# A two-layer MLP by Strassen-Winograd: one SBUF layout for both layers, twelve early quads, sums kept in DRAM

## Chip, core and metric

One core of one Trainium2 chip. The metric is the device time of one execution in microseconds (us); before: a median of 2001.36 over three runs (1999.55 to 2003.11).

## What is computed

One conformer convolution module and one squared-ReLU MLP, both with a residual, on 2048 tokens of width 1024 in fp32:

```python
def reference(x, ...):                     # x: (1, 2048, 1024)
    h = rms_norm(x, mix_norm[0])
    x = x + conformer_conv(h, ...)         # ends in ... @ w_out + b_out
    x = x + squared_relu_mlp(rms_norm(x, mlp_norm[0]), mlp_w1[0], mlp_w2[0])
    return x

def squared_relu_mlp(x, w1, w2):           # w1: 1024 x 4096, w2: 4096 x 1024
    return jnp.square(jax.nn.relu(x @ w1)) @ w2
```

## The kernel before

Everything is held transposed: features on the 128 partitions, 512 tokens a tile. The 2048 tokens are four blocks of 512. Every fp32 operand of a product is split into a high half (ACT casts it) and a low half (a subtraction on DVE or POOL), and a product takes three matmuls for each 128 of its depth: high by high, high by low, low by high. A tile of both halves is `act` (activations) or `wq` (weights, L559 to L563, from a raw tile `rawq`, 128 x 1024, 512 KB).

Blocks 0 and 1 are done first, with plain matmuls (the front, up to L531, 1188 us of the span); the conv outputs of blocks 2 and 3 are left in DRAM. The rest works on blocks 2 and 3 together, in phases, each with an SBUF pool of its own that takes the place of the one before (`reopened`):

- **Projection** (`project_spilled`): 16 loads of the conv outputs (`s`), each split; then for each block and each of eight row tiles a load of `w_out`, 24 matmuls into a `px` bank, and x + conv result goes to DRAM (`x2d`).
- **Norms**: `norm_first` and `norm_second` are generators. `poll()` in the matmul loop steps them, so that their instructions come between products; a number that they yield is how many of these turns they pause. They reload `x2d`, scale it and make seven forms (B11, B21, B22, T1 to T4) for Strassen-Winograd's products over the two blocks and the two halves of the width.
- **First layer**: 16 `Quad`s. Each takes a 2 x 2 block of `w1` tiles and makes seven products P1 to P7, 12 matmuls each, in PSUM banks `px` (3), `py` (2), `pz` (2); sums of products pass through squared ReLU and go to DRAM as forms of the hidden layer (`hB`, `hT`). The first `EARLY` quads do P1 and P2, which need only B11 and B21, while `norm_second` runs; P1's result goes to DRAM (`leave`) and comes back (`resume`) with P2's.
- **Second layer**: for g in 0..7 and o in 0, 1 (16 steps): `hidden(g)` loads and splits 14 tiles, `blocks(g, o)` loads four tiles of `w2` and forms seven weights, then 14 products of 6 matmuls. The results are added to sixteen accumulators `acc` in SBUF, by POOL (six adds a step, L850) and DVE (two, L864). After g = 7 they are stored to `outT`.

The order of instructions on an engine is set by a scheduler when the program is built, from the order of the code, priorities, and when buffers come free; every engine, and the DMA queue of SP, then runs its list in order. So a load that stands behind a store waits for what the store waits for.

Of the kernel before, what the change touches and what calls it, by code (L numbers as in the profile page):

```python
# [31 lines left out]
P = 128  # L32
# [6 lines left out]
T = 512  # L39
# [9 lines left out]
EARLY = 5  # L49
# [10 lines left out]
def conformer_mlp(ctx: ExitStack, tc, xT, w_in, w_out, w1, w2, vecs, conv_w, outT):  # L60
# [127 lines left out]

    class Stats:
# [9 lines left out]
        def buf(self, name, dtype=F32):  # L199
            tag, bufs = ("lstat", 3) if self.ln else ("stat", 4)  # L200
            return sb.tile([P, T], dtype, name=name, tag=tag, bufs=bufs)
# [394 lines left out]
    x2d = [[dram.tile([P, T], F32, name=f"x2_{b}_{m}") for m in range(KD)] for b in range(2)]  # L596
# [6 lines left out]
    def project_spilled(b, ss, norm):  # L603
        st = Stats(False)
        for m in range(KD):
            w = load_plain(w_out[m])
# [5 lines left out]
            nc.sync.dma_start(x2d[b][m], o)  # L612
            st.add_square(m, o)
        return spawn(norm(st))

    def x_normed(b, m, rs, xn):
        x = loaded(x2d[b][m], "x2")
# [8 lines left out]
    def norm_first(st):  # L626
        rs = yield from st.rstd_later(WAIT, GAP)
        for k in range(HK):
            n0[k] = acts.tile([P, 2, T], F32, name="n0", tag="act", bufs=n_act)
# [43 lines left out]
    class Quad:  # L673
# [12 lines left out]
        def sums(self):  # L686
            a2 = raw_wq(w1[2 * self.q + 1])
            a11, a12, a21, self.a22 = self.a1[:, :T], self.a1[:, T:], a2[:, :T], a2[:, T:]
            self.s1, self.s2 = small(sb, "s1", 1), small(sb, "s2", 1)
# [5 lines left out]
        def p1(self):  # L695
            product(self.x, w_split(self.a1[:, :T], nc.vector), form["B11"])
            self.c1 = small(wts, "p1", 2)
# [13 lines left out]
        def resume(self):  # L711
            self.high()
            self.c1 = small(wts, "p1", 2)
# [4 lines left out]
        def copied(self, ps, name):  # L718
            t = small(sb, name, 2)
# [24 lines left out]
        def p4(self):  # L744
# [7 lines left out]
            t1, t2, t4 = [small(sb, n, 1) for n in ("h1", "h2", "h4")]  # L752
# [14 lines left out]
    phase.close()  # L767
    sb, n_raw = reopened("first", phase), 4
# [24 lines left out]
    phase.close()  # L793
    sb = reopened("second", phase)
    ORDER = (("A11", "B11"), ("A12", "B21"), ("S2", "T2"), ("S1", "T1"), ("S3", "T3"), ("S4", "B22"), ("A22", "T4"))
    acc = [[None] * KD for _ in range(2)]

    def copied(ps, name, pool_=None):
        t = small(pool_ or sb, name, 2)
        nc.scalar.copy(t, ps)  # L800
        return t
# [29 lines left out]
    for g in range(NG):  # L831
        for o in range(2):
            if g == 0:
                for b in range(2):
                    for m in range(4 * o, 4 * o + 4, 2):
                        t = acts.tile([P, 2, T], F32, name="acc", tag="act", bufs=n_act)
                        for i in range(2):
                            acc[b][m + i] = t[:, i, :]
                            nc.sync.dma_start(acc[b][m + i], x2d[b][m + i])
# [3 lines left out]
            p1 = [copied(t, "p1", wts) for t in px]  # L843
            both(py, "P2", h["B21"], ws["A12"])
            c = [added(t, p) for t, p in zip(py, p1)]

            def add(x, n, ts):
                for i, t in enumerate(ts):
                    a = acc[n][4 * o + 2 * i + x]
                    nc.gpsimd.tensor_add(a, a, t)  # L850

            add(0, 0, c)
            both(px, "P6", h["T2"], ws["S2"], first=False)
            u2 = [copied(t, "u2") for t in px]
            both(pz, "P5", h["T1"], ws["S1"])
            p5 = [copied(t, "p5") for t in pz]
            both(px, "P7", h["T3"], ws["S3"], first=False)
            add(1, 1, [added(t, p) for t, p in zip(px, p5)])
            both(pz, "P3", h["B22"], ws["S4"], first=False)
            add(0, 1, [added(t, p) for t, p in zip(pz, u2)])  # L860
            both(px, "P4", h["T4"], ws["A22"], first=False)
            for i, t in enumerate(px):
                a = acc[0][4 * o + 2 * i + 1]
                nc.vector.tensor_add(a, a, t)  # L864
            if g == NG - 1:
                for m in range(4 * o, 4 * o + 4):
                    for b in range(2):
                        nc.sync.dma_start(outT[m * P : (m + 1) * P, (b + 2) * T : (b + 3) * T], acc[b][m])
# [51 lines left out]
```

## Time and profile before

| | |
|---|---|
| median of 3 runs | 2001.36 us |
| profiled execution | 2001.76 us, span 1999.6 us |
| busy: TensorE, DVE, ACT, POOL | 94%, 82%, 41%, 38% |
| mean granted TensorE clock | 0.978 of full speed |
| DMA | 264.60 MB, 132 GB/s over the span |

TensorE is the engine with most work. A row of the timeline gives the start, the time, the engine, the line, what is written and read, and in brackets how long the engine was idle before and what released it.

### The profile page before, as it was taken

Reading aid. Unit: us, or ns where it says so; the run is one execution under the profiler, and the core shown is the slowest. Engines: PE = TensorE matmul, PEld = TensorE weight load, DVE = VectorE, ACT = ScalarE, POOL = GpSimd, SP = SyncE. Lnnn points to the kernel's source line nnn. Section 1 sums busy time; section 2 is a strip of 40 time slices with the busy share of each in tenths; the row PEclk is TensorE's granted clock in tenths of the full one; section 3 lists DMA queues with packets and bytes.
Section 4 is the critical chain, followed back from the end, with each engine's and each line's share of the span. In section 5 each row is a group of like instructions: output and inputs, shape, how many; then the busy total and the mean of one; then the engine's idle time right before and its main releaser. Section 6 shows DMA issues by size and latency. Waiting matters only on the chain.

```text
span 1999.6 us, 23532 instructions
## 1 busy us (share of the span) xinstructions
PE 1883.3 (94%) x8192; PEld 1538.8 (77%) x8192; DVE 1640.7 (82%) x2315; ACT 820.4 (41%) x1322; POOL 751.3 (38%) x471
## 2 busy tenths in 40 slices
PE   8999999999899999999999977968999986999998
PEld 6888888888678778788888766856788875777777
DVE  7999999999999999799999733585656556899994
ACT  5323125243353333433231523443455554555552
POOL 2356322644445520000000003434444544676765
PEclk9999999999999999999999998988999998999999
DMA  5123222422224333643121456635545456444342
GB/s 198 64 88 116 89 76 75 143 96 96 89 89 138 106 111 111 219 143 99 62 70 64 155 188 224 225 129 189 191 142 169 157 193 205 156 143 143 122 136 84
DMA packets 135286, 264.60 MB, mean 132 GB/s; under 512 B 12928, under 2 KB 39680, under 8 KB 135168
## 3 DMA queue, kind: packets, MB, share of 16 engines
q1 hardware_dynamic: 135168, 263.11, 40.1%
q8 instruction: 64, 1.05, 0.2%
q14 instruction: 54, 0.44, 0.1%
HBM read 202.78 MB, written 60.28 MB: 132 GB/s over the span
## 4 chain that ended last, share of the span: by engine, by line
PE 40%; DVE 8%; issue 5%; DMA 4%; POOL 2%; ACT 1%; SPq 0%; POOLq 0%; DVEq 0%; ACTq 0%
PE ps L163 16%; PE px L586 11%; PE pz L586 5%; PE px L163 5%; PE py L586 3%; DVE act L93 2%; DVE wq L562 2%; DVE cc L665 1%; DMA rawq<-in_w 1%; DMA w2r<-in_w 1%; POOL s L814 1%; DVE acc L864 1%; ACT act L92 0%; POOL wq L562 0%; DMA s<-conv 0%
## 5 line engine op out<-in xcount | busy, mean ns | idle before, releaser
L163 PE MATMUL ps<-act,w 128*128 128x512 f32 x2880 | 666.2, 391 | 10.3 <-ACT w L92 7.9
L163 PEld LDWEIGHTS ps<-act,w 128*128 128x128 f32 x2880 | 541.4, 188 | 126.8 <-ACT w L92 7.9
L163 PE MATMUL ps<-hid,w 128*128 128x512 f32 x1920 | 445.6, 392 | 4.8 <-DVE hid L93 4.4
L163 PEld LDWEIGHTS ps<-hid,w 128*128 128x128 f32 x1920 | 360.0, 188 | 85.3 <-DVE hid L93 7.2
L586 PE MATMUL px<-act,wq 128*128 128x512 f32 x1536 | 375.5, 397 | 48.0 <-ACT wq L561 24.9
L586 PEld LDWEIGHTS px<-act,wq 128*128 128x128 f32 x1536 | 291.8, 191 | 116.8 <-ACT wq L561 25.8
L93 POOL TENSOR_TENSOR w<-raw,w 128x1024 fp32r<-128x1024 f32 x90 | 217.8, 2420 | 289.4 <-ACT w L92 282.7
L349 DVE SCALAR_TENSOR_TENSOR cacc<-hc,cw,cacc 128x512 f32<-128x512 f32 x464 | 324.7, 749 | 1.4
L349 DVE SCALAR_TENSOR_TENSOR cacc<-h,cw,cacc 128x512 f32<-128x512 f32 x464 | 316.8, 747 | 0.0
L92 ACT CAST w<-raw 128x1024 fp32r<-128x1024 f32 (+1 forms) x150 | 155.1, 1035 | 288.9 <-PE ps L163 284.3
L586 PE MATMUL pz<-act,wq 128*128 128x512 f32 x768 | 186.3, 392 | 2.1 <-ACT p L722 2.1
L850 POOL TENSOR_TENSOR acc<-acc,cc 128x512 f32<-128x512 f32 x96 | 149.5, 1575 | 89.1 <-DVE cc L665 77.2
L586 PEld LDWEIGHTS pz<-act,wq 128*128 128x128 f32 x768 | 145.4, 189 | 33.0 <-ACT p L722 2.5
L562 POOL TENSOR_TENSOR wq<-rawq,wq 128x512 fp32r<-128x512 f32 x48 | 72.8, 1517 | 148.7 <-ACT wq L561 144.8
L93 DVE TENSOR_TENSOR act<-ld,act 128x512 fp32r<-128x512 f32 x112 | 106.2, 971 | 15.8 <-ACT act L92 15.3
L562 DVE TENSOR_TENSOR wq<-rawq,wq 128x512 fp32r<-128x512 f32 x64 | 58.6, 917 | 70.0 <-ACT wq L561 70.0
L437 DVE TENSOR_TENSOR h<-h,ps 128x512 f32<-128x512 f32 x128 | 87.0, 684 | 31.1 <-PE ps L163 29.4
L163 PE MATMUL px<-act,wq 128*128 128x512 f32 x384 | 90.5, 398 | 22.8 <-ACT wq L561 22.8
L212 POOL TENSOR_TENSOR acc<-acc,hc 128x512 f32<-128x512 f32 x12 | 14.0, 1165 | 251.7 <-DVE hc L349 201.5
L586 PE MATMUL py<-act,wq 128*128 128x512 f32 x384 | 95.3, 398 | 13.7 <-DVE cc L665 13.7
L424 ACT ACTIVATE relu<-ps 128x512 f32<-128x512 f32 x64 | 38.2, 597 | 162.8 <-PE ps L163 159.1
L163 PEld LDWEIGHTS px<-act,wq 128*128 128x128 f32 x384 | 73.8, 193 | 39.0 <-ACT wq L561 23.3
(128 smaller groups left out, 2012.7 us busy)
## 6 DMA issues: line engine op xcount, KB each, us to landing
raw<-in_w SPq DMA_DIRECT2D x104, 512.0 KB, 3.6
rawq<-in_w SPq DMA_DIRECT2D x37, 512.0 KB, 4.2
xt<-in_xT SPq DMA_DIRECT2D x64, 256.0 KB, 3.6
ld<-hT SPq DMA_DIRECT2D x64, 256.0 KB, 3.0
w2r<-in_w SPq DMA_DIRECT2D x64, 256.0 KB, 3.8
raw<-in_w_in SPq DMA_DIRECT2D x30, 512.0 KB, 3.2
hB<-cc SPq DMA_DIRECT2D x48, 256.0 KB, 3.6
ld<-hB SPq DMA_DIRECT2D x48, 256.0 KB, 3.8
```

What stands on the lines that cost most here:

```text
L92: nc.scalar.copy(hl[:, 0, :], src)
L93: eng.tensor_sub(hl[:, 1, :], src, hl[:, 0, :].bitcast(F32))
L163: nc.tensor.matmul(ps, lhsT=w(k, a), rhs=x[:, b, :], start=k == 0 and i == 0, stop=k == len(xs) - 1 and i == 2,)
L349: nc.vector.scalar_tensor_tensor(out, h[:, k : k + T], cw[:, j, k : k + 1], acc, ALU.mult, ALU.add)
L424: nc.scalar.activation(r, ps, AF.Relu)
L437: nc.vector.tensor_add(x2[i][m], x2[i][m], ps)
L562: eng.tensor_sub(hl[:, 1, :], src, hl[:, 0, :].bitcast(F32))
L586: nc.tensor.matmul(ps, lhsT=hl[:, a, off + k * P : off + (k + 1) * P], rhs=x[:, b, :], start=first and k == 0 and i == 0, stop=k == n - 1 ...
L665: nc.vector.tensor_add(out, ps, t)
L814: nc.gpsimd.tensor_add(s1, a21, a22)
L850: nc.gpsimd.tensor_add(a, a, t)
L864: nc.vector.tensor_add(a, a, t)
```

## The change

Five things change, all behind the front:

- `EARLY` goes from 5 to 12. `norm_second` pauses four turns instead of one, writes B22 over B11, and makes all low halves on DVE (before, T1 and B22 on POOL).
- The pools of the three phases become one set (`low`, `wts`, `high`, `mid`, `top`, `sb2`) that is open throughout. Small tiles share a tag of six buffers, `rawq` has four, and results that wait for a later product share four buffers of 128 x 2 x 512 (`pair`).
- The first weights of the projection and the first eight `s` tiles are loaded with priority; the other eight come after the first block's projection in the code.
- The second layer loads `w2` as two tiles of 512 KB instead of four of 256 KB; its first step forms its weight sums on DVE.
- The sums stay in DRAM (`x2_pairs`): for g < 7 GpSimd issues DMAs that add a pair tile to them (`accum_op`), four a step, and no accumulator is in SBUF; P4 is copied out of PSUM by ACT. For g = 7 the sum so far is loaded (`base`), DVE and POOL add the last results, and it is stored. The descriptor scratch space of DMAs is halved (8192).

```diff
-EARLY = 5
+EARLY = 12
...
-    wts = reopened("wts", ctx)
-    forms = ctx.enter_context(ExitStack())
-    acts = reopened("acts", forms)
-    n_act, n_raw, n_tmp = 29, 2, 2
-    phase = ctx.enter_context(ExitStack())
-    sb = reopened("projection", phase)
+    low, wts, high, mid, top, sb = [reopened(n, ctx) for n in ("low", "wts", "high", "mid", "top", "sb2")]
...
+    def mid_tile(name):
+        return mid.tile([P, T], F32, name=name, tag="m", bufs=6)
...
+    def pair(name):
+        return sb.tile([P, 2, T], F32, name=name, tag="pair", bufs=4)
...
     def raw_wq(src):
-        t = sb.tile([P, 2 * T], F32, name="rawq", tag="rawq", bufs=n_raw)
-        nc.sync.dma_start(t, src)
+        t = top.tile([P, 2 * T], F32, name="rawq", tag="rawq", bufs=4)
+        nc.sync.dma_start(t if src.shape == t.shape else t.rearrange("p (s q c) -> p s q c", s=2, q=2), src)
         return t
...
     def norm_second(st):
         rs = yield from st.rstd_later(WAIT, GAP)
         for k in range(HK):
-            b12 = x_normed(1, k, rs, small(sb, "n1", 3))
-            b22 = x_normed(1, HK + k, rs, small(sb, "n1", 3))
             b11, b21 = n0[k][:, 0, :], n0[k][:, 1, :]
-            t1 = small(sb, "t1", 1)
+            b12 = x_normed(1, k, rs, mid_tile("n1"))
+            t1, t2 = mid_tile("t1"), mid_tile("t2")
             nc.vector.tensor_sub(t1, b12, b11)
-            t2 = small(sb, "t2", 1)
+            b22 = x_normed(1, HK + k, rs, b11)
             nc.vector.tensor_sub(t2, b22, t1)
             form["T2"][k] = act_split(t2)
-            form["T1"][k] = act_split(t1, nc.gpsimd)
-            yield 1
+            form["T1"][k] = act_split(t1)
+            yield 4
             nc.vector.tensor_sub(b12, b22, b12)
             form["T3"][k] = act_split(b12)
-            form["B22"][k] = act_split(b22, nc.gpsimd)
             nc.vector.tensor_sub(b21, b21, t2)
-            form["T4"][k] = act_split(b21)
-            yield 1
-
-    ss = [[act_split(loaded(conv_out[j][i], "s")) for j in range(KD)] for i in range(2)]
-    ta = project_spilled(0, ss[0], norm_first)
-    tb = project_spilled(1, ss[1], norm_second)
+            yield 4
+        for k in range(HK):
+            form["B22"][k] = act_split(n0[k][:, 0, :])
+            form["T4"][k] = act_split(n0[k][:, 1, :])
+            yield 4
+
+    with tc.high_priority():
+        w0 = load_plain(w_out[0])
+        ss = [act_split(loaded(conv_out[j][0], "s")) for j in range(KD)]
+    ta = project_spilled(0, ss, norm_first, w0)
+    ss = [act_split(loaded(conv_out[j][1], "s")) for j in range(KD)]
+    tb = project_spilled(1, ss, norm_second)
     finish(ta)
...
-        a11, a12, a21, a22 = [small(sb, "w2r", 8) for _ in range(4)]
-        for i, t in enumerate((a11, a12, a21, a22)):
-            nc.sync.dma_start(t.rearrange("p (q c) -> p q c", q=2), w2[g, o][:, i])
-        s1, s2 = small(sb, "s1", 1), small(sb, "s2", 1)
-        nc.gpsimd.tensor_add(s1, a21, a22)
-        nc.gpsimd.tensor_sub(s2, s1, a11)
+        a1, a2 = [raw_wq(w2[g, o][:, 2 * i : 2 * i + 2]) for i in range(2)]
+        a11, a12, a21, a22 = a1[:, :T], a1[:, T:], a2[:, :T], a2[:, T:]
+        s1, s2 = mid_tile("s1"), mid_tile("s2")
+        eng = nc.gpsimd if g or o else nc.vector
+        eng.tensor_add(s1, a21, a22)
+        eng.tensor_sub(s2, s1, a11)
...
+            end = g == NG - 1
+
+            def out(x, n, ts, t):
+
+                at = x2_pairs[n][2 * o + x]
+                if end:
+                    base = pair("c")
+                    nc.sync.dma_start(base, at)
+                c = t if t is not None and not end else pair("c")
+                for i, ps in enumerate(ts):
+                    if t is not None:
+                        nc.vector.tensor_add(c[:, i, :], ps, t[:, i, :])
+                    elif end:
+                        nc.vector.tensor_add(base[:, i, :], ps, base[:, i, :])
+                    else:
+                        nc.scalar.copy(c[:, i, :], ps)
+                    if end:
+                        m = 4 * o + 2 * i + x
+                        if t is not None:
+                            nc.gpsimd.tensor_add(base[:, i, :], base[:, i, :], c[:, i, :])
+                        nc.sync.dma_start(outT[m * P : (m + 1) * P, (n + 2) * T : (n + 3) * T], base[:, i, :])
+                if not end:
+                    nc.gpsimd.dma_start(at, c, accum_op=ALU.add)
...
             both(py, "P2", h["B21"], ws["A12"])
-            c = [added(t, p) for t, p in zip(py, p1)]
...
-            add(0, 0, c)
+            out(0, 0, py, p1)
...
             both(px, "P4", h["T4"], ws["A22"], first=False)
-            for i, t in enumerate(px):
-                a = acc[0][4 * o + 2 * i + 1]
-                nc.vector.tensor_add(a, a, t)
-            if g == NG - 1:
-                for m in range(4 * o, 4 * o + 4):
-                    for b in range(2):
-                        nc.sync.dma_start(outT[m * P : (m + 1) * P, (b + 2) * T : (b + 3) * T], acc[b][m])
+            out(1, 0, px, None)
...
-    nc = bacc.Bacc("TRN2", target_bir_lowering=False, num_devices=1)
+    nc = bacc.Bacc("TRN2", target_bir_lowering=False, num_devices=1, dynamic_dma_scratch_size=8192)
```

In order, on the DMA queue of SP, where the projection begins (`s` are the conv outputs of blocks 2 and 3, `rawq` the weights): before,

```order
241 L575 DMA s<-conv_1_121 128x512
242 L575 DMA s<-conv_1_123 128x512
243 L575 DMA s<-conv_1_125 128x512
244 L575 DMA s<-conv_1_127 128x512
245 L567 DMA rawq<-in_w_out 128x1024
246 L575 DMA xt<-in_xT 128x512
```

and in the changed kernel

```order
228 L442 DMA outT<-h 128x512 x11
229 L590 DMA rawq<-in_w_out 128x1024
230 L598 DMA s<-conv_0_112 128x512
231 L598 DMA s<-conv_0_114 128x512
232 L598 DMA s<-conv_0_116 128x512
233 L598 DMA s<-conv_0_118 128x512
234 L598 DMA s<-conv_0_120 128x512
235 L590 DMA rawq<-in_w_out 128x1024
236 L598 DMA s<-conv_0_122 128x512
237 L598 DMA s<-conv_0_124 128x512
238 L598 DMA s<-conv_0_126 128x512
```

The first weight load went from behind the sixteen `s` loads to ahead of them all.

On DVE, in `norm_second` (`n`, `t` are its tiles; `cc<-py,p` is the add behind P2 that frees P2's bank; `wq` is a weight split of an early quad): before,

```order
942 L641 TENSOR_TENSOR t_10468<-n_10460,n_9902 128x512
943 L93 TENSOR_TENSOR act<-n_9883,act 128x512
944 L618 SCALAR_TENSOR_TENSOR n_10464<-x_10465,vec,rstd 128x512
945 L618 SCALAR_TENSOR_TENSOR n_10495<-x_10496,vec,rstd 128x512
946 L643 TENSOR_TENSOR t_10470<-n_10464,t_10468 128x512
947 L647 TENSOR_TENSOR n_10460<-n_10464,n_10460 128x512
948 L650 TENSOR_TENSOR n_9902<-n_9902,t_10470 128x512
949 L93 TENSOR_TENSOR act<-t_10470,act 128x512
950 L93 TENSOR_TENSOR act<-n_10460,act 128x512
951 L641 TENSOR_TENSOR t_10503<-n_10495,n_9921 128x512
952 L93 TENSOR_TENSOR act<-n_9902,act 128x512
954 L665 TENSOR_TENSOR cc<-py,p_10451 128x512
```

and in the changed kernel

```order
953 L646 SCALAR_TENSOR_TENSOR n_10515<-x_10516,vec,rstd 128x512
954 L585 TENSOR_TENSOR wq<-rawq,wq 128x512
955 L668 TENSOR_TENSOR t_10519<-n_10515,n_9903 128x512
956 L697 TENSOR_TENSOR cc<-py,p_10541 128x512
957 L646 SCALAR_TENSOR_TENSOR n_9903<-x_10522,vec,rstd 128x512
958 L585 TENSOR_TENSOR wq<-rawq,wq 128x512
959 L670 TENSOR_TENSOR t_10520<-n_9903,t_10519 128x512
960 L674 TENSOR_TENSOR n_10515<-n_9903,n_10515 128x512
961 L676 TENSOR_TENSOR n_9903<-n_9903,t_10520 128x512
962 L93 TENSOR_TENSOR act<-t_10520,act 128x512
963 L93 TENSOR_TENSOR act<-t_10519,act 128x512
964 L93 TENSOR_TENSOR act<-n_10515,act 128x512
```

Before, the norm's instructions stand in one piece ahead of the early quads' last adds; now each `k` of the norm has a quad's splits and its add in between.

On POOL, in two steps of the second layer (`acc` are accumulators, `s` the weight sums of L814 and L815, now L842 and L843, `x_` the sums in DRAM): before,

```order
284 L814 TENSOR_TENSOR s_14933<-w2r 128x512
285 L815 TENSOR_TENSOR s_14934<-s_14933,w2r 128x512
286 L850 TENSOR_TENSOR acc<-acc,cc 128x512 x2
287 L562 TENSOR_TENSOR wq<-w2r,wq 128x512
288 L850 TENSOR_TENSOR acc<-acc,cc 128x512 x4
289 L814 TENSOR_TENSOR s_15160<-w2r 128x512
```

and in the changed kernel

```order
235 L585 TENSOR_TENSOR wq<-rawq,wq 128x512
236 L883 DMA x_0_0_9328<-p_13445 128x1024
237 L842 TENSOR_TENSOR s_13756<-rawq 128x512
238 L843 TENSOR_TENSOR s_13757<-s_13756,rawq 128x512
239 L883 DMA x_1_1_9333<-p_13490 128x1024
240 L883 DMA x_1_0_9332<-u_13475 128x1024
241 L883 DMA x_0_1_9329<-c 128x1024
242 L585 TENSOR_TENSOR wq<-rawq,wq 128x512
```

Six adds a step became four DMA issues, each of which waits for its pair tile; the sums for the next step stand between the first and the second of them.

## Rows read from the trace of the kernel before

**Rows 1.** The page: busy us of each engine (PEld: its weight loads), share of the span, instructions.

```profile
PE 1883.3 (94%) x8192; PEld 1538.8 (77%) x8192; DVE 1640.7 (82%) x2315; ACT 820.4 (41%) x1322; POOL 751.3 (38%) x471
```

**Rows 2.** By stretch: length, busy time by engine (instructions), granted clock, DMA share, GB/s.

```profile
0.00:1180.00 1180.00, 1155.06 (x5068) 944.90 (x5069) 1079.26 (x1615) 422.56 (x630) 331.74 (x191) 1.00 0.34 111
...
1211.00:1302.00 91.00, 91.00 (x396) 75.09 (x395) 40.67 (x64) 35.68 (x60) 40.04 (x30) 0.97 0.66 222
1302.00:1345.00 43.00, 29.34 (x126) 23.89 (x125) 36.81 (x56) 20.49 (x38) 14.26 (x10) 0.85 0.31 103
...
1630.00:1660.00 30.00, 14.31 (x55) 11.00 (x53) 11.19 (x13) 10.65 (x19) 9.90 (x7) 0.77 0.77 258
```

**Rows 3.** Waits of TensorE: line, releaser, us in total, times, longest.

```profile
PE px L586 <- ACT wq L561: 24.9, 2, 14.1
PE px L163 <- ACT wq L561: 22.8, 1, 22.8
PE px L586 <- DVE acc L864: 18.7, 14, 2.9
PE py L586 <- DVE cc L665: 13.7, 1, 13.7
```

**Rows 4.** Timeline, 1185 to 1216, the projection's start.

```profile
1188.72 14.63 SPq L575 DMA_DIRECT2D s<-conv  x16
...
1203.41 0.42 SPq L567 DMA_DIRECT2D rawq<-in_w_out  x1
...
1210.43 5.87 PE L163 MATMUL px<-act,wq 128*128 128x512 f32 x13 [22.84 <-ACT wq L561]
```

**Rows 5.** Timeline, 1325 to 1362, the end of the early quads.

```profile
1341.46 5.02 PE L586 MATMUL py<-act,wq 128*128 128x512 f32 x12 [13.66 <-DVE cc L665]
...
1357.27 4.94 PE L586 MATMUL px<-act,wq 128*128 128x512 f32 x10 [10.80 <-ACT wq L561]
```

**Rows 6.** Timeline of TensorE, 1395 to 1407 and 1634 to 1725.

```profile
1403.93 3.33 PE L586 MATMUL px<-act,wq 128*128 128x512 f32 x7 [2.77 <-DVE cc L665]
...
1639.03 4.62 PE L586 MATMUL pz<-act,wq 128*128 128x512 f32 x12 [2.08 <-ACT p L722]
...
1660.52 5.49 PE L586 MATMUL px<-act,wq 128*128 128x512 f32 x12 [14.13 <-ACT wq L561]
...
1668.99 2.88 PE L586 MATMUL px<-act,wq 128*128 128x512 f32 x12
1671.71 2.88 PE L586 MATMUL pz<-act,wq 128*128 128x512 f32 x12
```

**Rows 7.** Timeline of SP's queue, 1636 to 1662.

```profile
1653.44 1.84 SPq L812 DMA_DIRECT2D w2r<-in_w  x4
```

**Rows 8.** Timeline, 1985 to 2000, the last DVE add.

```profile
1994.82 0.69 DVE L864 TENSOR_TENSOR acc<-acc,px 128x512 f32<-128x512 f32 x1 [0.67 <-PE px L586]
```

**Rows 9.** Groups by line, 1720 to 1995: busy us, mean ns, idle before.

```profile
L850 POOL TENSOR_TENSOR acc<-acc,cc 128x512 f32<-128x512 f32 x83 | 129.9, 1583 | 74.5 <-DVE cc L665 74.2
...
L93 DVE TENSOR_TENSOR act<-ld,act 128x512 fp32r<-128x512 f32 x77 | 70.2, 934 | 1.8 <-ACT act L92 1.8
...
L815 POOL TENSOR_TENSOR s<-s,w2r 128x512 f32<-128x512 f32 x12 | 20.7, 1722 | 0.9
L562 POOL TENSOR_TENSOR wq<-w2r,wq 128x512 fp32r<-128x512 f32 x13 | 20.1, 1548 | 12.3 <-ACT wq L561 12.3
...
L814 POOL TENSOR_TENSOR s<-w2r 128x512 f32<-128x512 f32 x12 | 17.8, 1482 | 0.0
...
L800 ACT COPY p<-pz 128x512 f32<-128x512 f32 x28 | 16.5, 589 | 9.1 <-PE pz L586 8.7
```

**Rows 10.** DMA queue of the span; issues with landing, whole span, then 1660 to 1995.

```profile
q1 hardware_dynamic: 135168, 263.11, 40.1%
...
rawq<-in_w SPq DMA_DIRECT2D x37, 512.0 KB, 4.2
...
acc<-x SPq DMA_DIRECT2D x8, 256.0 KB, 5.7
```

More of the change, by code (lines that the diff above doesn't have):

```diff
@@ L187, in x_tile, with stat_buf @@
         return stream("xt", xT[k * P : (k + 1) * P, b * T : (b + 1) * T])
+    def stat_buf(ln, name, dtype):
+        tag, bufs = ("lstat", 3) if ln else ("stat", 4)
+        return sb.tile([P, T], dtype, name=name, tag=tag, bufs=bufs)
     class Stats:
@@ L199, in buf @@
         def buf(self, name, dtype=F32):
-            tag, bufs = ("lstat", 3) if self.ln else ("stat", 4)
-            return sb.tile([P, T], dtype, name=name, tag=tag, bufs=bufs)
+            return stat_buf(self.ln, name, dtype)
         def add(self, k, t, eng=None):
@@ L542, in conformer_mlp, with act_tile, tmp, stat_buf @@
     psp = reopened("psb", ctx, space=PSUM)
-    wts = reopened("wts", ctx)
-    forms = ctx.enter_context(ExitStack())
-    acts = reopened("acts", forms)
-    n_act, n_raw, n_tmp = 29, 2, 2
-    phase = ctx.enter_context(ExitStack())
-    sb = reopened("projection", phase)
+    low, wts, high, mid, top, sb = [reopened(n, ctx) for n in ("low", "wts", "high", "mid", "top", "sb2")]
+    n_act = {"low": 16, "high": 13}
+    taken = [0]
+    def act_tile(name="act"):
+        n = taken[0] % 29
+        taken[0] += 1
+        side = "high" if n < 13 else "low"
+        pool_ = high if n < 13 else low
+        return pool_.tile([P, 2, T], F32R, name=name, tag=side, bufs=n_act[side])
+    def mid_tile(name):
+        return mid.tile([P, T], F32, name=name, tag="m", bufs=6)
+    def tmp(name, ln=False):
+        return mid_tile(name)
+    def pair(name):
+        return sb.tile([P, 2, T], F32, name=name, tag="pair", bufs=4)
+    def stat_buf(ln, name, dtype):
+        return sb.tile([P, 2, T], dtype, name=name, tag="pair", bufs=4)[:, 0, :]
+    def pair_tile(name):
+        return pair(name)[:, 0, :]
     def xbank():
@@ L594, in product, with x2d @@
             poll()
-    x2d = [[dram.tile([P, T], F32, name=f"x2_{b}_{m}") for m in range(KD)] for b in range(2)]
+    x2_pairs = [[dram.tile([P, 2, T], F32, name=f"x2_{b}_{m}") for m in range(KD // 2)] for b in range(2)]
+    def x2d(b, m):
+        return x2_pairs[b][m // 4 * 2 + m % 2][:, m // 2 % 2, :]
     def load_plain(src):
@@ L616, in x_normed @@
     def x_normed(b, m, rs, xn):
-        x = loaded(x2d[b][m], "x2")
+        x = loaded(x2d(b, m), "x2")
         nc.vector.scalar_tensor_tensor(xn, x, v(V_MLP + m), rs, ALU.mult, ALU.mult)
@@ L628, in norm_first @@
         for k in range(HK):
-            n0[k] = acts.tile([P, 2, T], F32, name="n0", tag="act", bufs=n_act)
+            n0[k] = act_tile("n0").bitcast(F32)
             for y in range(2):
@@ L751, in p4 @@
             c11, c12, c22 = self.c11, self.c12, self.c22
-            t1, t2, t4 = [small(sb, n, 1) for n in ("h1", "h2", "h4")]
+            t1, t2, t4 = [mid_tile(n) for n in ("h1", "h2", "h4")]
             nc.gpsimd.tensor_sub(t1, c12, c11)
@@ L766, in conformer_mlp @@
     finish(tb)
-    phase.close()
-    sb, n_raw = reopened("first", phase), 4
     last = None
@@ L790, in conformer_mlp, with copied @@
     last.p4()
-    phase.close()
-    sb = reopened("second", phase)
     ORDER = (("A11", "B11"), ("A12", "B21"), ("S2", "T2"), ("S1", "T1"), ("S3", "T3"), ("S4", "B22"), ("A22", "T4"))
[L796 to L800, printed above, removed]
+    def copied(ts, name):
+        t = pair(name)
+        for i, ps in enumerate(ts):
+            nc.scalar.copy(t[:, i, :], ps)
         return t
@@ L832, in conformer_mlp @@
         for o in range(2):
-            if g == 0:
-                for b in range(2):
[L835 to L839, printed above, removed]
+            end = g == NG - 1
[5 more added lines that the diff above has]
+                c = t if t is not None and not end else pair("c")
+                for i, ps in enumerate(ts):
+                    if t is not None:
[11 more added lines that the diff above has]
+                    nc.gpsimd.dma_start(at, c, accum_op=ALU.add)
             ws = blocks(g, o)
@@ L842, in conformer_mlp @@
             both(px, "P1", h["B11"], ws["A11"])
[L843 removed]
+            p1 = copied(px, "p1")
             both(py, "P2", h["B21"], ws["A12"])
[L845 to L852 removed]
+            out(0, 0, py, p1)
             both(px, "P6", h["T2"], ws["S2"], first=False)
[L854 removed]
+            u2 = copied(px, "u2")
             both(pz, "P5", h["T1"], ws["S1"])
[L856 removed]
+            p5 = copied(pz, "p5")
             both(px, "P7", h["T3"], ws["S3"], first=False)
[L858 removed]
+            out(1, 1, px, p5)
             both(pz, "P3", h["B22"], ws["S4"], first=False)
[L860 removed]
+            out(0, 1, pz, u2)
             both(px, "P4", h["T4"], ws["A22"], first=False)
[L862 to L868 removed]
+            out(1, 0, px, None)
             if o == 0 and g < NG - 1:
```

14 lines of the change are left out of this document (7 added, 7 removed).

## The prediction, made before the changed kernel ran

> **What bounds the kernel now.** I read the page first. TensorE is busy 94% of the span [rows 1], so time can come only from its 116 us of idling and from stretches at the lower clock. The table by stretch says where these lie: up to 1180 us, which the change doesn't touch, TensorE idles 25 us, and from 1211 to 1302 it never stops [rows 2]. The rest sits at seams and in the second layer. Third, TensorE's waits: two on weight casts (24.9 us), one on the first weight cast of the projection (22.8), one on the DVE add of P2 (13.7), and fourteen on the accumulator add of L864 (18.7) [rows 3]. The timelines around these show what is late.
>
> *Seam 1, 1187.6 to 1210.4.* SP issues all sixteen `s` loads, which takes 14.63 us, and only then the first weights of the projection, at 1203.41. TensorE starts at 1210.43 after 22.84 us [rows 4].
>
> *Seam 2, 1327.8 to 1357.3, and once more at 1403.93.* DVE is busy 36.81 of 43 us from 1302 to 1345 [rows 2] with `norm_second`, ahead of the add that frees P2's bank. TensorE waits 13.66, then 10.80 for the first sums of the first resumed quad, whose `rawq` tiles belong to the pool opened next, and 2.77 for the last early quad's [rows 5, 6]. After each wait it runs slowly for about twelve matmuls: 12 in 5.02 us, against 12 in 2.88 otherwise [rows 5, 6].
>
> *Seam 3, 1636 to 1660.* 2.08 us, then 14.13: the second layer's first weights are issued at 1653.44, after the hidden tiles of the last quad [rows 6, 7]. In this stretch the granted clock is 0.77 [rows 2].
>
> *Second layer.* A step is 84 matmuls. Twelve take 2.72 us (the starts at 1668.99 and 1671.71 [rows 6]), so 16 steps want 304.6 us. They take from 1660.52 to about 1994.7, 334.2 us. Beyond them come 4.9 us: the last DVE adds and the store [rows 8]. Of the 29.6 us too much, 2.6 are the slow first twelve, 18.7 the waits on L864, which frees the `px` bank, 1.6 one early wait, the rest slow matmuls behind the waits. L864 is late because DVE works beside POOL, whose 83 accumulator adds take 1.58 us each and stand ahead of the weight sums of L814 and L815 [rows 9].
>
> **The change, part by part.** The profiled execution took 2001.76 us for a span of 1999.6, 0.4 above the median 2001.36. The sum is made against it.
>
> *(a) Weights ahead of the `s` tiles.* The `rawq` load now stands where the first `s` load stood, 1188.72. It lands 4.2 us later (median of `rawq`, [rows 10]); its first halves are split 1.3 us later (one cast of 0.6, one subtraction of 0.7), so the first matmul comes at 1194.2, 16.2 us earlier. It then trickles with the `s` tiles: ten issues at 0.91 (14.63/16) end at 1197.9, and with 4.2 for landing (the `rawq` figure for want of better) and 1.3 for the split the eighth tile is there at about 1203. Before, the projection's first 24 matmuls ended at 1210.43 + 5.87 + 11 x 0.227 = 1218.8. Gain 15; bounds 10 (loads slowed by one another) and 16.2. The other eight tiles are split under the next 43 us of matmuls.
>
> *(b) Twelve early quads, `norm_second` spread.* Early work is now 24 products, 65.3 us of TensorE. Under it DVE has per quad two splits and an add (2.1 us, 25 in all), and per `k` two scalings, four subtractions and five splits at 0.7 (7.6, 30 in all): 55 of 65 us, with POOL silent beside it. So the 13.66, and with ready forms and no new pool the 10.80 and 2.77, should go: 27.2, and with them the slow matmuls, (5.02 - 2.88) + (4.94 - 2.43) + (3.33 - 1.75) = 6.2. I leave 4 us, since several casts and adds now stand between pieces of `norm_second` and a product of TensorE waits for each; what it leaves over, DVE has 10 us to absorb. Gain 29.4; bounds 6 and 33.4. The seven more spilled P1 and reloads go by DMA: a resumed quad moves twelve tiles' worth, 3.15 MB in 13.6 us, 231 GB/s. The projection ran without a gap at 222 [rows 2], so I price it at nothing; if that fails, it is a rival below.
>
> *(c) One layout.* The second layer's weights and sums no longer wait for a pool to close. The 2.08 and 14.13 and their slow matmuls, (4.62 - 2.88) + (5.49 - 2.88) = 4.4, are 20.6. I keep 3 of it, because the last quad's own tiles must still be stored and read again: 17.6; bounds 8 and 20.6.
>
> *(d) Sums in DRAM.* Per step six POOL adds (9.5 us) and two DVE adds (1.4) go; ACT gets two copies of 0.59 [rows 9], to 10.5 or so of 19, on the path to the bank, where a shorter queue stands than DVE's. POOL gets four accumulating DMAs of 512 KB. No transfer that adds is in the trace, so it is bounded. Below by a plain one: 263.11 MB in 40.1% of the span [rows 10] is 328 GB/s, 1.6 us of all engines. A step's loads are 2.88 MB, 8.8 us; with four plain transfers 15.2 of 19.04, 80%. Above by a load and a store of the same bytes, 3.2 each: 21.6. I take the plain end for the time, since the bytes that leave SBUF are those, but leave 0.5 of the 1.34 us per step waiting, as landing times grow at 80%: 11.7 of 18.7, and 5 of the slow matmuls. Gain 16.7; bounds -6 (below) and 27.
>
> The row puts the price at 1.6 us. The Trainium skill (Collectives: The Full Stack, "The bandwidth ceiling: the fold count and why AG ≠ RS ≠ AR") says that a transfer which adds reads two sources for one write, and runs at half the rate for that. No run here shows it yet. By it the sum would be that of the first rival.
>
> *(e) Last two steps.* Here POOL adds, DVE adds and `outT` stores all pass through the four pair buffers, and a base must be loaded into one that a store has left. Before, this end was 4.9 us. I add 4; bounds 0 and 12.
>
> Sum: 15 + 29.4 + 17.6 + 16.7 - 4 = 74.7, so **1927**. If everything goes at the good bounds it is 1905: only the untouched part and 3072 back-half matmuls are left.
>
> **The rivals.**
> 1. *Accumulating costs a read of the destination besides.* Then a step needs 21.6 us of the DMA engines for 19.04 of matmuls, 14 steps 302.4, and with the last two 340.5: 6.3 more than before instead of 16.7 less. 1950. For it: the engines must fetch both operands. Against: 328 GB/s is no measured ceiling.
> 2. *Resumed quads wait.* Twelve instead of five reload P1 and P2's result, and DMA is at the rate of the busiest stretch. If each waits as the one at 1403.93 did, 2.77: 33 us, 1960. Against: loads are issued a quad ahead.
> 3. *DVE is too full in the early stage.* Its 55 of 65 us become over 65 if its operations run at 0.9 (as those of [rows 9] do beside POOL). The waits of seam 2 come back but for the four I left: 1950.
> 4. *Slower: POOL's queue is held by its DMAs.* If an issue keeps POOL until the transfer is through, a step costs POOL 4t plus a sum, a difference and a split (1.48 + 1.72 + 1.55 [rows 9]). At t = 5.7, the landing of the accumulators' loads [rows 10], that is 27.6 us a step, 424 for the layer: 2033. It decides from t = 5.1 on. Below 3.6 it costs nothing. Against: other queues' issues take 0.3 to 0.5. The Trainium skill (DMA: Bandwidth & Descriptors, "SWDGE vs HWDGE vs iDMA") says that for DMAs issued from GpSimd a program on GpSimd itself computes the descriptors; how long that holds its queue for these, no run here shows.
>
> **How the numbers follow.** The forecast 0.45 (its own range 1908 to 1942, from its bounds), rival 1 0.25, rival 2 0.1, rival 3 0.08, rival 4 0.08; 0.04 for a mixture that cancels. Measurements of this kernel lie 0.2% apart, so 0.2%, 4 us, is what can be told from no change. Faster 0.88, same 0.03, slower 0.09. The range 1904 to 1962 holds the first four cases down to the good bounds and leaves rival 4 out.
>
> **What would show it.** (a) First matmul of the projection near 1194, its first 24 ending near 1203. (b) No wait of TensorE over 3 us between 1290 and 1390, and the granted clock above 0.95 there. (c) No gap before the second layer beyond some 3 us. (d) Steps of 19.5 us, a DMA share near 0.8, POOL's DMA issues short. If DMA share nears 1 and steps take 21 or more, rival 1 holds; if TensorE waits for a `wq` split by POOL, whose queue stands at a DMA, rival 4. What would make me wrong altogether is a wait in the steady second layer: it counts fourteen times, so one of 5 us takes the whole gain.

## The result and the profile after

The changed kernel took 2015.67 us (median of six runs, 2008.22 to 2018.67) against 2002.23 for the kernel before: a ratio of 1.0063, 95% interval 1.0043 to 1.0083. It is slower by 0.6%, where 1927 and faster was forecast. The profiled execution has a span of 2006.5 us, 6.9 more than before; it took 2008.22 us, the shortest of the six, so readings from it account for 6.9 of the 13.4 us between the medians.

The page: busy time, then the DMA queues (packets, MB, share of the time of 16 engines). `q0` is the queue of the transfers that GpSimd issues.

```profile
PE 1894.8 (94%) x8192; PEld 1546.0 (77%) x8192; DVE 1605.4 (80%) x2318; ACT 826.8 (41%) x1336; POOL 649.6 (32%) x433
...
q1 hardware_dynamic: 133440, 272.28, 40.6%
q0 software_dynamic: 8064, 29.36, 8.3%
```

POOL lost 102 us of work and DVE 35, and TensorE is no better for it. The waits of TensorE say where to look (line, releaser, us, times, longest):

```profile
PE px L609 <- DVE p L872: 47.7, 14, 7.2
...
PE px L163 <- ACT act L92: 7.1, 1, 7.1
...
PE py L609 <- DVE cc L697: 2.9, 1, 2.9
```

The seams went nearly as forecast: one wait of 7.1 for 22.8 at the projection, one of 2.9 for the 13.7 and 10.8 at the norm [rows 3, 5]. The 18.7 on L864 [rows 3] became 47.7 on L872, the DVE adds of the second layer. The timeline at the seams:

```profile
1191.22 0.38 SPq L590 DMA_DIRECT2D rawq<-in_w_out  x1
...
1197.18 0.80 PE L163 MATMUL px<-act,wq 128*128 128x512 f32 x1 [7.14 <-ACT act L92]
...
1333.22 0.73 PE L609 MATMUL py<-act,wq 128*128 128x512 f32 x2 [2.87 <-DVE cc L697]
...
1600.83 5.73 PE L609 MATMUL px<-act,wq 128*128 128x512 f32 x24
...
1611.48 4.69 PE L609 MATMUL px<-act,wq 128*128 128x512 f32 x12 [2.19 <-ACT wq L584]
```

The last twelve of the 24 from 1600.83 are the first product of the second layer, so it begins at 1600.83 + 12 x 0.227 = 1603.6; before it began at 1660.52 [rows 6]. That is 57 us earlier. The second layer then runs to 1997.7 (the start at 1994.86 of the last twelve, and 2.88): 394.1 us for 334.2 before, 59.9 more; and 8.8 us follow its end for 4.9, 3.9 more. -57 + 59.9 + 3.9 = 6.8, the whole difference of the spans. The table by stretch (length, busy time, granted clock, DMA share, GB/s) shows the same: a nearly full TensorE up to the second layer, then 47 to 51 of 60 us between 1660 and 1900, with DMA engines at 0.77 to 0.84 (four of the rows):

```profile
1302.00:1345.00 43.00, 40.13 (x169) 32.46 (x169) 39.90 (x66) 30.76 (x57) 0.00 (x0) 0.96 0.54 181
...
1404.00:1500.00 96.00, 96.00 (x425) 79.50 (x425) 83.06 (x85) 46.42 (x77) 64.52 (x42) 1.00 0.71 234
...
1660.00:1720.00 60.00, 50.55 (x211) 40.66 (x210) 32.84 (x49) 29.96 (x54) 18.68 (x17) 0.94 0.84 210
...
1780.00:1840.00 60.00, 48.67 (x194) 38.99 (x195) 34.53 (x53) 27.80 (x50) 18.30 (x17) 0.90 0.77 184
```

One of the long waits, in the timeline of 1740 to 1790:

```profile
1763.24 3.80 SPq L590 DMA_DIRECT2D rawq<-in_w  x2
...
1776.67 1.25 POOL L842 TENSOR_TENSOR s<-rawq 128x512 f32<-128x512 f32 x1 [8.98 <-DMA rawq<-in_w]
1777.96 0.69 DVE L847 TENSOR_TENSOR rawq<-rawq 128x512 f32<-128x512 f32 x1 [10.73 <-POOL s L842]
...
1781.56 1.28 DVE L872 TENSOR_TENSOR p<-px,p 128x512 f32<-128x512 f32 x2
1782.30 7.16 PE L609 MATMUL px<-act,wq 128*128 128x512 f32 x24 [6.29 <-DVE p L872]
```

Read from the bottom. TensorE's P4 waits for the DVE add of P7 (L872), which must read the bank before P4 goes on in it. That add had its input since P7 ended at 1773.3, but stands on DVE behind a weight difference (L847), which idled DVE for 10.73 us, waiting for POOL's sum (L842), and that for a weight load that came late. And this load is no concern of the present step. The order on POOL shown ahead of the prediction has `s_13756` in the step of `p_13445`. Tiles are numbered in the order of the code; P1's tiles of three steps running are `p_13445`, `p_13658`, `p_13801`, and the sums 13756 and 13757 go with the last. So the sum, the difference and their load belong to the step after next, and not to the next, as it was put there. On DVE the difference (on `rawq_13754`) stands between the adds of P2 (`p_13445`) and those of P7 (`p_13490`). Waits of DVE and POOL in 1660 to 1950:

```profile
DVE rawq L847 <- POOL s L842: 87.4, 12, 11.7
POOL s L842 <- DMA rawq<-in_w: 73.0, 12, 9.9
```

And why the load is late, by the DMA view of the same stretch (290 us):

```profile
q0 software_dynamic: 6825, 24.81, 47.6%
q1 hardware_dynamic: 13536, 30.94, 30.7%
...
rawq<-in_w SPq DMA_DIRECT2D x24, 512.0 KB, 8.4
x<-p POOLq DMA_DIRECT2D x24, 512.0 KB, 7.6
```

The adding transfers hold the engines for 0.476 x 290 / 24.81 = 5.56 us a MB, 2.92 us for 512 KB; the loads beside them for 2.88 us a MB, 1.51. Loads of 512 KB land after 8.4 us, where `rawq` took 4.2 before [rows 10].

### The profile page after: what moved, and what is told of

It reads as the page before. It is cut to its first block, busy times and chain, and to the rows that moved or that the text cites. A ratio compares the mean times of both kernels' runs of the same rounds, so it can differ in the third digit from the quotient of the medians.

```text
span 2006.5 us, 23614 instructions
## 1 busy us (share of the span) xinstructions
PE 1894.8 (94%) x8192; PEld 1546.0 (77%) x8192; DVE 1605.4 (80%) x2318; ACT 826.8 (41%) x1336; POOL 649.6 (32%) x433
## 3 DMA queue, kind: packets, MB, share of 16 engines
q0 software_dynamic: 8064, 29.36, 8.3%
HBM read 210.12 MB, written 91.47 MB: 150 GB/s over the span
## 4 chain that ended last, share of the span: by engine, by line
PE 37%; issue 9%; DVE 5%; DMA 5%; POOL 3%; ACT 2%; SPq 0%; DVEq 0%; POOLq 0%; ACTq 0%
PE ps L163 16%; PE px L609 12%; PE pz L609 4%; PE py L609 3%; PE px L163 2%; DVE wq L585 1%; POOL x L883 1%; DVE act L93 1%; DMA s<-conv 1%; DMA rawq<-in_w_out 1%; POOL s L842 1%; DMA ld<-hT 1%; DVE p L872 1%; DMA c<-x 1%; ACT act L92 1%
## 5 line engine op out<-in xcount | busy, mean ns | idle before, releaser
L609 PE MATMUL px<-act,wq 128*128 128x512 f32 x1536 | 386.1, 405 | 61.3 <-DVE p L872 47.7
L609 PEld LDWEIGHTS px<-act,wq 128*128 128x128 f32 x1536 | 299.5, 196 | 134.6 <-DVE p L872 53.6
L585 DVE TENSOR_TENSOR wq<-rawq,wq 128x512 fp32r<-128x512 f32 x128 | 123.2, 969 | 68.5 <-ACT wq L584 68.5
L584 ACT CAST wq<-rawq 128x512 fp32r<-128x512 f32 x192 | 117.9, 620 | 124.1 <-DMA rawq<-in_w_out 38.7
L585 POOL TENSOR_TENSOR wq<-rawq,wq 128x512 fp32r<-128x512 f32 x64 | 92.4, 1444 | 236.2 <-ACT wq L584 164.9
L93 DVE TENSOR_TENSOR act<-ld,act 128x512 fp32r<-128x512 f32 x112 | 82.6, 756 | 22.7 <-ACT act L92 22.1
L163 PE MATMUL px<-act,wq 128*128 128x512 f32 x384 | 89.9, 395 | 7.7 <-ACT act L92 7.1
L92 ACT CAST act<-ld 128x512 fp32r<-128x512 f32 x112 | 69.0, 620 | 61.3 <-DMA ld<-hB 27.8
```

The lines of the kernel that those rows point to most:

```text
L92: nc.scalar.copy(hl[:, 0, :], src)
L93: eng.tensor_sub(hl[:, 1, :], src, hl[:, 0, :].bitcast(F32))
L163: nc.tensor.matmul(ps, lhsT=w(k, a), rhs=x[:, b, :], start=k == 0 and i == 0, stop=k == len(xs) - 1 and i == 2,)
L584: nc.scalar.copy(hl[:, 0, :], src)
L585: eng.tensor_sub(hl[:, 1, :], src, hl[:, 0, :].bitcast(F32))
L609: nc.tensor.matmul(ps, lhsT=hl[:, a, off + k * P : off + (k + 1) * P], rhs=x[:, b, :], start=first and k == 0 and i == 0, stop=k == n - 1 ...
```

## The experiments

Two theories. **Price**: an adding transfer holds the DMA engines about twice as long as a plain one, and so makes the loads land late. **Queue**: the wait comes from the order on DVE, where an operation of the step after next (some expectations call it the next step's) stands ahead of an add that TensorE needs now. Twelve kernels follow: seven bear on these two, one on the early quads, and four use what they show. Each ratio is to the kernel before, measured beside it on the same chip, so times of different groups of runs are compared by their ratios.

### Plain stores in place of adding transfers

```diff
-                    nc.gpsimd.dma_start(at, c, accum_op=ALU.add)
+                    nc.gpsimd.dma_start(at, c)
```

> The changed kernel with the 56 transfers of the second layer as plain stores (the sums are not formed, so the output lacks them); bytes, queue and waits stay. Price theory (an adding transfer holds the DMA engines about twice as long as a plain one, 2.9 us against 1.5, and that makes the weight loads land at 8.4 us instead of 4): the software queue's share of the DMA engines falls from 8.3% to about 4.3, weight loads land in about 5 us, the waits of TensorE on the DVE add of L872 fall from 47.7 us to under 15, and the time to 1940 to 1955. Queue theory (the DVE add of P7 stands behind the next step's weight difference, which is late whatever the transfers cost, because its load is issued late): the waits stay above 30 us and the time above 1985.

1963.01 us, ratio 0.9837 (0.9823 to 0.9852). `q0` moves the same 29.36 MB in 4.0% of the engines' time, half of 8.3%. But the waits on L872 fell only from 47.7 to 26.0 us, and the time stayed above the band of the price theory and below that of the queue theory. Both have a part. The order of instructions on every engine is that of the changed kernel.

### Sums in SBUF, in the new layout

```diff
+                        t = low.tile([P, 2, T], F32, name="acc", tag="low", bufs=16)
+                        nc.sync.dma_start(t, x2_pairs[n][2 * o + x])
...
-                    nc.gpsimd.dma_start(at, c, accum_op=ALU.add)
+                        nc.gpsimd.tensor_add(a[:, i, :], a[:, i, :], t[:, i, :])
```

> The changed kernel with the sums kept in SBUF as before (eight accumulators of 128 x 2 x 512 in the pool of the forms, six POOL adds and two DVE adds a step, no adding transfer). Price theory: the second layer takes what it took before, 334 us from its first matmul, which the changed kernel reaches at 1611 instead of 1660; with the old tail of 5 us 1950 of span, a time of 1950 to 1958. Layout theory (the shared buffers and the 512 KB weight loads of the new layout lengthen the second layer by themselves): a step stays above 22 us and the time above 1975.

1968.94 us, 0.9869 (0.9854 to 0.9884): faster than before by 1.3%, with all that the change did to the seams and none of its DRAM sums. In time it lies between the two bands; its steps are as the layout theory had them. The waits at 1704.36 and at 1883.25 are eight steps apart, 22.4 us a step, where the second layer before took 20.9 (334.2/16). So in the new layout a step is some 1.5 us longer even without the transfers. (Here and in all kernels below with sums in SBUF, 21 tiles are left for split activations instead of 29, since accumulators take the others.) TensorE's waits in it:

```profile
PE px L609 <- DVE acc L880: 20.0, 7, 3.6
PE px L609 <- DVE p L877: 11.2, 8, 4.3
```

The first is what was 18.7 before [rows 3]; the second is new.

### Priority for the adds

```diff
+                        with tc.high_priority():
                             nc.vector.tensor_add(c[:, i, :], ps, t[:, i, :])
```

> The changed kernel with the DVE adds of the second layer (L872) given priority by the scheduler, so that P7's add no longer stands behind the next step's weight difference; the adding transfers stay. Queue theory: TensorE's waits on L872 fall from 47.7 us to under 15, a step from 25 us to about 21, where four transfers of 2.9 us and loads of 8.3 us fill the DMA engines; time 1945 to 1965. Price theory in its strong form (the DMA engines are full, and any order only moves the wait): a step stays at 24 us or more, with the wait moved to a weight split, time above 1995.

2011.88 us, 1.0084 (1.0069 to 1.0099), waits on these adds 45.5. This decides nothing: in the order that came out, the difference still stands ahead of P7's add. On DVE only two adds, those of P2 in the first step, changed places.

### Five early quads again

```diff
-EARLY = 12
+EARLY = 5
```

> The changed kernel with EARLY back at 5, everything else as changed. If the twelve early quads are what covers the second norm, TensorE waits again some 20 to 35 us between 1300 and 1380 and the time is 2035 to 2050. If the one layout and the norm's new order do it, the time stays within 8 us of the changed kernel's 2016.

2026.53 us, 1.0155 (1.0138 to 1.0173), 0.9% above the changed kernel's ratio, and in time between the two bands. The wait is back at the end of the early quads:

```profile
PE px L609 <- ACT wq L584: 20.2, 2, 16.7
```

16.7 us in one piece, a little less than the 20 expected. The seven more early quads are worth some 18 us, and the 231 GB/s of the resumed quads cost nothing: the changed kernel ran from 1404 to 1500 without a gap at 234.

### The difference moved to POOL

```diff
-        nc.vector.tensor_sub(a21, a11, a21)
+        nc.gpsimd.tensor_sub(a21, a11, a21)
```

> The changed kernel with one subtraction a step (L847, the weight difference for S3) moved from DVE to POOL, behind POOL's two weight sums, on which it waits anyway. In the changed kernel's order it belongs to the step after next, waits for a weight load that has only just been issued, and stands on DVE ahead of the add of P7, for which TensorE waits. Queue theory: TensorE's waits on L872 fall from 47.7 us to under 15, a step from 25 us to 20 to 21.5, the time to 1945 to 1968. Price theory in its strong form (the DMA engines are full, 11.8 us of adding transfers and 8.3 of loads a step): steps stay at 23 us or more, the wait shows at a weight split or a copy instead, time above 1990.

1988.39 us, 0.9945 (0.9926 to 0.9964). One subtraction on another engine makes the changed kernel faster than the one before. TensorE's waits on L872 are 1.9 us, as the queue theory says. But a step still takes 23.7 us (1699.43 to 1889.21 for eight) and the wait shows at a copy, as the price theory says; the time is between the two bands, 1.6 us below the price theory's. Another engine that works in order has become the place where a late load is waited for. The timeline, and TensorE's waits:

```profile
1793.05 0.62 ACT L92 CAST act<-ld 128x512 fp32r<-128x512 f32 x1 [6.01 <-DMA ld<-hT]
1793.58 0.58 ACT L828 COPY p<-pz 128x512 f32<-128x512 f32 x1
...
1794.21 2.93 PE L609 MATMUL pz<-act,wq 128*128 128x512 f32 x6 [5.45 <-ACT p L828]
```

```profile
PE pz L609 <- ACT p L828: 36.1, 12, 6.5
```

ACT's copy of P5 stands behind the cast of a hidden tile of the next g, whose load took its time.

### The same move with sums in SBUF, and with plain stores

The same line is changed in the second and in the first kernel above.

> The kernel with sums in SBUF (1969 us) with the same subtraction moved to POOL. Queue theory: its waits on the adds of L877 (11.2 us) go, those on L880 (20.0), behind DVE's work beside POOL's adds, stay: 1952 to 1962. If POOL, which now has ten operations of about 1.5 us a step, becomes late instead: 1970 or more.

> The kernel with plain stores in place of the adding transfers (1963 us; the sums are not formed) with the same subtraction moved to POOL. Queue theory: its 26.0 us of waits on L872 fall under 8, 1925 to 1938; the difference to the run that keeps the adding transfers and has the same move is then what the price of adding costs by itself, 10 to 30 us. If the waits come from full DMA engines, 1955 or more.

With sums in SBUF: 1968.74 us, 0.9849 (0.9822 to 0.9877), no change that can be told, and in neither band. The waits on L877 are 15.2 us and those on L880 18.4: here DVE is late by its own work (217 of 250 us busy, in 1680 to 1930), not for a load. With plain stores: 1936.32 us, 0.9682 (0.9655 to 0.9709), as the queue theory had it; the price of adding by itself, expected at 10 to 30 us, comes out larger (below). From 1680 to 1880 TensorE hardly stops; the DMA view of that stretch gives the plain price:

```profile
1680.00:1880.00 200.00, 199.27 (x874) 163.37 (x873) 143.12 (x202) 124.48 (x223) 86.24 (x84) 1.00 0.73 250
```

```profile
q0 software_dynamic: 6014, 21.88, 30.0%
...
rawq<-in_w SPq DMA_DIRECT2D x20, 512.0 KB, 6.1
```

0.300 x 200 / 21.88 = 2.74 us a MB, 1.44 us for 512 KB, against 2.92 for the adding ones. The four kernels make a square of ratios:

| | adding transfers | plain stores |
|---|---|---|
| difference on DVE | 1.0063 | 0.9837 |
| difference on POOL | 0.9945 | 0.9682 |

Moving the difference is worth 0.012 and 0.016 (24 and 31 us), making the transfers plain 0.023 and 0.026 (45 and 52 us), each about the same with and without the other. In each row of the square the order of instructions is the same on every engine.

### Each result stored twice, plainly

```diff
                     nc.gpsimd.dma_start(at, c)
+                    nc.gpsimd.dma_start(again[n][2 * o + x], c)
```

> The run with plain stores and the subtraction on POOL (1936 us), each result stored twice, to two places in DRAM: eight plain transfers of 512 KB a step, which hold the DMA engines as long as four adding ones (the sums are not formed). If engine time is what an adding transfer costs, this comes out like the run with four adding transfers: 1975 to 1995, DMA share 0.8 to 0.9, waits on ACT's copies. If adding costs by something else (the order in which it reads and writes one place, its place among the queues), it stays under 1955.

1977.73 us, 0.9901 (0.9887 to 0.9915). Twice the plain bytes cost 0.022 of the 0.026 that adding costs, with the same wait of TensorE on ACT's copy of P5 (26.1 us in all, for 36.1) and the same DMA share as with four adding transfers, 0.84 in 1680 to 1930:

```profile
1680.00:1930.00 250.00, 222.22 (x929) 180.12 (x928) 146.40 (x209) 129.71 (x233) 111.20 (x133) 0.94 0.84 307
```

So most of the price of adding is engine time. 307 GB/s were moved here; the adding kernel with the same share moved 206.

### Fewer adding transfers

Of the four results of a step one (P4's), two (and P3's) or three (and P7's) go by an adding transfer, the rest into accumulators in SBUF; the difference is on POOL. (The kernel with one is written a little otherwise, to the same effect. The kernel with four has 29 tiles for split activations, the others 21.)

```diff
+                kept = (x, n) in KEPT
...
+                        if kept or end:
+                            nc.gpsimd.tensor_add(a[:, i, :], a[:, i, :], t[:, i, :])
...
+                if not end and not kept:
+                    nc.gpsimd.dma_start(x2_pairs[n][2 * o + x], c, accum_op=ALU.add)
```

> Sums of three results of a step in SBUF with POOL's adds, the fourth (P4) copied out of PSUM by ACT and added in DRAM by one transfer; the subtraction on POOL as well. One adding transfer a step takes 2.9 of 19 us, and DVE, which is late beside POOL, loses the two adds behind which TensorE waits in the run with all sums in SBUF. If both readings hold, the waits on DVE's adds fall under 10 us: 1938 to 1950. If POOL is too full (16 of 19 us a step), 1965 or more.

> Two results of a step (P2 and P7) summed in SBUF by four POOL adds, two (P3 and P4) by adding transfers, the subtraction of L847 on POOL. The DMA engines get 5.9 us of adding transfers and 8.3 of loads a step, 14.2 of 19, as full as with four plain stores, where TensorE hardly waited; POOL is relieved by two adds, DVE of the adds into accumulators. Price theory: 1940 to 1955, faster than with all sums in SBUF (1969) and than with one adding transfer (1960). If the landing times of the loads matter at this share already, 1960 to 1975.

> One result of a step (P2) summed in SBUF, three by adding transfers, the subtraction of L847 on POOL. DMA engines 8.8 + 8.3 = 17.1 of 19 us a step. Price theory: between two (below 1955) and four adding transfers (1988): 1955 to 1975, with waits of TensorE on ACT's copies, which stand behind casts of late loads. If what costs in the run with four is something else than their number, within 5 us of 1988 or of the run with two.

| adding transfers a step | 0 | 1 | 2 | 3 | 4 |
|---|---|---|---|---|---|
| ratio | 0.9849 | 0.9805 | 0.9833 | 0.9875 | 0.9945 |
| DMA share, 1680 to 1930 | 0.38 | 0.53 | 0.67 | 0.74 | 0.84 |
| DVE busy of 250 us | 217 | 229 | 210 | 168 | 147 |

One (1959.72, interval 0.9774 to 0.9836) is in neither band, with 15.5 us of waits on DVE's adds where under 10 was expected. Two (1961.09, 0.9812 to 0.9854) missed the price theory's band and came in the other, by which landing times matter at this share already. One and two can't be told apart. Three came in its own band (1972.39, 0.9857 to 0.9894). To the left TensorE waits for DVE, to the right for late loads, and in the middle for both. With two, ACT is still held up by hidden tiles, the longest time for 9.2 us:

```profile
ACT act L92 <- DMA ld<-hT: 46.4, 15, 9.2
```

### Two adding transfers, eight hidden loads under way

```diff
-            out[n] = [act_split(loaded(hid_d[2 * g + k][n])) for k in range(2)]
+            t = low.tile([P, 2, T], F32, name="ld", tag="low", bufs=16)
+            for k in range(2):
+                nc.sync.dma_start(t[:, k, :], hid_d[2 * g + k][n])
+            out[n] = [act_split(t[:, k, :]) for k in range(2)]
```

> The run with two results summed in SBUF and two by adding transfers (1961 us), with the hidden tiles loaded into four tiles of double size that are free there, so that eight loads can be under way instead of five. In that run TensorE waits 24 us on ACT's copies out of PSUM, which stand behind a cast of a hidden tile whose load lands up to 9 us late. If the load is late because it is issued late, those waits fall under 10 us and the time to 1943 to 1954. If it is late because the DMA engines are full, the time stays at 1957 to 1965.

1951.18 us, 0.9775 (0.9755 to 0.9795): the fastest kernel here that forms the sums, 2.2% below the one before and in its band, though its interval overlaps that of one adding transfer. ACT's wait for these tiles fell from 46.4 to 11.5 us, and those of TensorE on ACT's copies in the second layer from 24 to 15.6 (6.6, 4.7 and 4.3), where under 10 was expected:

```profile
PE pz L609 <- ACT p L828: 6.6, 2, 3.7
...
PE px L609 <- ACT p L828: 4.7, 3, 2.1
PE px L609 <- ACT u L828: 4.3, 2, 2.2
```

The DMA share in 1680 to 1930 is 0.67 with five and with eight loads under way. So most of ACT's wait came of tiles asked for late, for want of buffers.

## Why the prediction was wrong, step by step

**(a) Weights ahead of the `s` tiles: right.** The front ended 2.45 us later in this execution (1190.04 for 1187.59). From there the first matmul came 15.7 us earlier (13.25 + 2.45) for 16.2, and the first 24 ended near 1206.4, where the DVE add that waits for them starts: 12.4 + 2.45 = 14.9 us for 15.

**(b) and (c), the two other seams: right in mechanism, a little too much.** Forecast for (a) to (c) were 62 us; the second layer began 57 earlier, 59.4 from the end of the front. The waits went as told: of 66.3 us at the seams 12.4 remain ahead of the second layer (7.14, 0.52, 2.87, 1.89), and 2.19 in its first step. Mis-sized were the slow matmuls behind them: TensorE's busy time from the end of the front to the start of the second layer is 406.7 us before (1187.6 to 1660.5) and 400.9 after (1190.04 to 1603.55), so 5.7 of the 10.6 us credited there came. The rival "DVE is too full in the early stage" did not come about: one wait of 2.87, at the place where the order mixes casts and products. "Resumed quads wait" did not either.

**(d) Sums in DRAM: the step that failed.** Forecast was a gain of 16.7, and "I take the plain end for the time, since the bytes that leave SBUF are those". The second layer became 59.9 us longer. Two things were wrong in it.

*The price.* 2.92 us a transfer, not 1.6; the upper bound, 3.2, was close. The Trainium skill (Collectives: The Full Stack, "The bandwidth ceiling: the fold count and why AG ≠ RS ≠ AR") says of the reduce step of a collective that its add needs two source reads, and so runs at half the rate; the prediction carried that over to any transfer that adds. The trace agrees in size: 2.92 against 1.44 to 1.51 us. That a second read is the cause is not shown: the profile counts 210.12 MB read from HBM with adding and with plain stores alike. Not the price alone but its form as engine time is shown, for most of it, by the kernel that stores twice. It makes 45 to 52 us.

*The queue.* Rival 1 had the right price and came out at 1950, because it let the DMA engines' throughput set the step: 21.6 us. A step took 25.0 (1681.88 to 1881.97 for eight), and the engines were at 0.77 to 0.84, not full. The prediction said of L864 that it is late because of POOL's adds, and took the wait to go with them; it did not look for what would stand ahead of the adds of P2, P7 and P3 on DVE. There stood a difference for the step after next, which waits for a load issued in this one, and it held DVE for up to 11.7 us, twelve times. Before, the same difference (L819) cost DVE 12.8 us in 1720 to 1995:

```profile
L819 DVE TENSOR_TENSOR w2r<-w2r 128x512 f32<-128x512 f32 x12 | 8.2, 686 | 12.8 <-POOL s L814 12.8
```

Two things differed there. The loads, of 256 KB, landed in 3.8 us instead of 8.4. And the difference stood elsewhere: in every other step ahead of the adds of P2, for the next step, and in the rest behind the adds of P7, between the two of P3; never two steps early and ahead of P7's. So the new place in the order came with the change too; what each of the two counts for is not shown. Moving the difference was worth 24 us with adding transfers and 31 with plain stores. Both together, price and place, are 1.0063 - 0.9682, 76 us. By the two profiles (d) was wrong by 16.7 + 59.9 - 4.4 = 72.2, since 4.4 us of the second layer are a wait that belongs to (e). The prediction's last sentence named such a wait as what would overturn it, but not its place.

**Rival 4, POOL's queue held by its DMAs: wrong.** An issue took POOL 0.86 to 0.88 us (medians of the three groups; the longest 1.24), against the 5.1 from which it would decide:

```profile
L883 POOL DMA_DIRECT2D x<-p x28: 875/877/1062, 1617.0 to 1949.9; - x28
L883 POOL DMA_DIRECT2D x<-u x14: 862/862/881, 1631.6 to 1951.4; - x14
L883 POOL DMA_DIRECT2D x<-c x14: 862/864/1242, 1632.8 to 1954.3; - x14
```

**(e) The end: right in mechanism, half its size.** 8.8 us behind the last matmul for 4.9, as the base of the last result is loaded only when a store has left its buffer; 4 were taken. But in the last two steps TensorE also waits 4.4 us for DVE's add of P4, which waits for such a base. So it cost 8.3, within the bounds of 0 and 12:

```profile
1978.30 1.29 DVE L874 TENSOR_TENSOR c<-px,c 128x512 f32<-128x512 f32 x2 [3.18 <-DMA c<-x]
1979.04 2.17 PE L609 MATMUL px<-act,wq 128*128 128x512 f32 x6 [4.35 <-DVE c L874]
```

What stays open: why a step with all sums in SBUF takes 22.4 us in the new layout and 20.9 in the old one. DVE is no busier in it (212 of 250 us, 1680 to 1930, against 216 of 240, 1740 to 1980), and the move of the difference did not change it. It was not tried with the old four weight tiles. Nor were eight hidden loads tried with four adding transfers.

## What to carry to other kernels

When a transfer is made dearer, the bill is not only its share of the DMA engines but, as here, what every other load's landing time does to queues that work in order; look on each engine for an operation that needs a late load and stands ahead of one that TensorE needs, and at how far ahead of its use it stands. A load for two steps ahead did harm here because its first consumer was queued before this step's adds: put such a consumer on an engine that has nothing urgent behind it, as with the difference, or give the loads more buffers, as with the hidden tiles. And when a change bundles several gains, time it with the doubtful part taken out: here the change without its DRAM sums was worth 1.3%, and one moved subtraction decided the sign.

## Not expected of the hardware

At one and the same DMA share, 0.84, the engines moved 206 GB/s with adding transfers and 307 with twice the plain stores: here the share of busy time alone does not give the bytes. And the traffic of the resumed quads, 234 GB/s, cost TensorE nothing, where a second layer at 184 to 210 GB/s stood for about a sixth of its time (the rows of 1660 and 1780).
